# Feed-forward input products as seven half-size products for eight, in a two-layer encoder kernel

## The chip, the cores and the metric

The kernel runs on one core of one Trainium2 chip. The metric is device time in microseconds of one execution, the median of three runs. TensorE multiplies matrices, VectorE and ScalarE work element by element, GpSimd does a little of the same, and SyncE issues all transfers from main memory.

## The reference

512 tokens of width 1024 pass through two layers. Layer 0 mixes tokens with two kinds of heads, layer 1 with an mLSTM. Each is followed by the feed-forward part that this change is about:

```python
def conv_glu_ffn(h, w_in, conv_w, conv_b, w_out):
    u = jnp.matmul(h, w_in)              # (512, 1024) x (1024, 2 * 2816)
    a, g = jnp.split(u, 2, axis=-1)
    a = causal_dwconv(a, conv_w, conv_b) # 3 taps along the tokens
    return jnp.matmul(jax.nn.gelu(a) * g, w_out)

x = x + g_f * conv_glu_ffn(modulate(x, norm_ffn_g, sh_f, sc_f), ...)
```

The modulation (shift, scale, gate) of each sub-layer is a product of `c` with `ada_w`, 6 x 1024 columns for each layer.

## The kernel before

Activations lie transposed: a tile holds 128 channels in its partitions and 512 tokens along it. Every matmul takes 32-bit operands in a rounded form (`F32R`). To keep the precision each operand is split in a high part and a low part, and `mm3` issues three products: high by high, high by low, low by high. Weights are split on chip, in `load_split`: SyncE loads a raw piece of 128 x 2048, ScalarE rounds it to the high part (line 212), VectorE subtracts to get the low part (line 213). There are two raw buffers and three pairs of high and low.

The feed-forward part (`ffn`) has 22 tiles of 128 channels for `a` and 22 for `g`. They are made two at a time (a pair): 8 slices of the 1024 inputs, times two tiles, times `a` and `g`, times three products, is 96 matmuls of 128 x 512. The first pair is done in two halves of 256 tokens, because the second half of the tokens is normalized while the first is multiplied (`Handoff`, `modulate`). Behind the products of a tile stands a chain of its own: ScalarE (line 1038), two taps on VectorE (1040, 1042), GELU on ScalarE (1047), the product with `g` on VectorE (1048), and the split (219, 220). After 8 tiles their output product is added to `x` (8 blocks, `x_update`, line 351), after 16 again, and the last 6 go through `halves_out`, which ends the layer in two halves of 256 tokens and feeds the next norm.

The modulation columns (`ada_many`, line 170) are VectorE reductions over 128 x 1024 raw weights, 96 of them in the kernel. They are put between other work: 24 in the mixer of layer 0 (after 16 at its start), 48 in the feed-forward part of layer 0, 8 in that of layer 1.

A scheduler sets the order on each engine from the dependencies and the program's order; each engine then runs its list strictly in that order. Tile pools decide when a buffer is free.

## Time and profile before

| what | us |
|---|---|
| median of 3 runs | 1295.5 (1294.74 to 1295.51) |
| the profiled execution, its own time | 1296.03 |
| its span, first to last instruction | 1294.3 |
| TensorE busy | 1261.4 |
| VectorE busy | 797.7 |
| ScalarE busy | 471.9 |

The busy time of an engine is the union of its instructions. Matmuls overlap: the time that one adds is the distance between the starts of two that follow each other, not its duration.

### The profile page before, as it was taken

What the parts mean: (1) busy time and instruction counts of PE and PEld (TensorE: products, weight loads), DVE (VectorE), ACT (ScalarE), POOL (GpSimd) and SP (SyncE); (2) the same over time, 40 slices, a digit from 0 to 9 for tenths busy, and PEclk for the clock granted to TensorE, in tenths of its full rate; (3) what the DMA queues carried; (4) which work ended last, traced back from release to release, by engine and by line L of the source; (5) the groups of instructions that cost most, each with busy time, mean ns of one, the idle gap of its engine ahead of it and who ended that gap; (6) DMA issues with size and microseconds to landing.
All of it is one profiled execution on the core that took longest, in us unless ns stands there. A gap on an engine that the chain in (4) does not pass through costs nothing.

```text
span 1294.3 us, 16057 instructions
## 1 busy us (share of the span) xinstructions
PE 1261.4 (97%) x6390; PEld 1046.6 (81%) x6390; DVE 797.7 (62%) x1213; ACT 471.9 (36%) x734; POOL 114.4 (9%) x199
## 2 busy tenths in 40 slices
PE   5999999999999999999999999999999999999997
PEld 4866788899888888888898777779988888888887
DVE  7845678757865477447665846567875335443555
ACT  4454323125321132212346665774522122221321
POOL 0022154401000000000000120111000000000000
PEclk9999999999999999999999999999999999999998
DMA  8832635221664356434423203111162313222221
GB/s 316 293 105 82 212 98 195 87 77 66 218 206 143 128 204 225 146 130 159 169 91 128 78 21 104 59 66 66 66 212 70 126 65 125 71 100 96 82 74 66
DMA packets 33242, 162.47 MB, mean 126 GB/s; under 512 B 3600, under 2 KB 6032, under 8 KB 21648
## 3 DMA queue, kind: packets, MB, share of 16 engines
q1 hardware_dynamic: 33168, 161.46, 36.6%
q8 instruction: 50, 0.82, 0.3%
q14 instruction: 24, 0.20, 0.0%
HBM read 159.35 MB, written 2.10 MB: 125 GB/s over the span
## 4 chain that ended last, share of the span: by engine, by line
PE 86%; issue 7%; DVE 2%; POOL 2%; DMA 1%; ACT 1%; SPq 0%; POOLq 0%; DVEq 0%; ACTq 0%
PE acc L224 20%; PE acc L226 20%; PE acc L225 20%; PE mx L225 5%; PE mx L224 5%; PE mx L226 5%; PE mx L455 2%; PE acc L260 1%; PE acc L262 1%; PE acc L261 1%; PE mx L859 1%; PE mx L885 1%; PE mx L500 1%; DMA wraw<-wflat 1%; PE mx L550 1%
## 5 line engine op out<-in xcount | busy, mean ns | idle before, releaser
L224 PE MATMUL acc<-hh,wah 128*128 128x512 f32 (+1 forms) x384 | 145.0, 378 | 0.1
L226 PE MATMUL acc<-hh,wgl 128*128 128x512 f32 (+1 forms) x384 | 144.7, 377 | 0.0
L226 PE MATMUL acc<-hh,wal 128*128 128x512 f32 (+1 forms) x384 | 144.5, 376 | 0.0
L224 PE MATMUL acc<-hh,wgh 128*128 128x512 f32 (+1 forms) x384 | 144.3, 376 | 0.0
L225 PE MATMUL acc<-hl,wgh 128*128 128x512 f32 (+1 forms) x384 | 144.2, 376 | 0.0
L225 PE MATMUL acc<-hl,wah 128*128 128x512 f32 (+1 forms) x384 | 144.1, 375 | 0.0
L170 DVE CUSTOM_DVE_ANT_0 adaraw<-adaraw,csb,par 128x1024 f32<-128x1024 f32 x96 | 123.5, 1289 | 2.3 <-DMA adaraw<-adaT 2.3
L213 DVE TENSOR_TENSOR wl<-wraw,wh 128x2048 fp32r<-128x2048 f32 (+1 forms) x40 | 87.2, 2179 | 50.1 <-ACT wh L212 50.0
L224 PE MATMUL acc<-hh,wh 128*128 128x512 f32 x256 | 104.9, 410 | 0.0
L226 PE MATMUL acc<-hh,wl 128*128 128x512 f32 x256 | 101.4, 396 | 0.0
L225 PE MATMUL acc<-hl,wh 128*128 128x512 f32 x256 | 101.4, 396 | 0.0
L225 PE MATMUL mx<-actl,wdh 128*128 128x512 f32 x256 | 101.2, 395 | 0.0
L224 PE MATMUL mx<-acth,wdh 128*128 128x512 f32 x256 | 101.1, 395 | 0.0
L226 PE MATMUL mx<-acth,wdl 128*128 128x512 f32 x256 | 100.8, 394 | 0.0
L212 ACT CAST wh<-wraw 128x2048 fp32r<-128x2048 f32 (+1 forms) x40 | 72.0, 1801 | 64.8 <-PE acc L225 59.2
L212 ACT CAST wgh<-wgraw 128x2048 fp32r<-128x2048 f32 x22 | 42.0, 1907 | 139.5 <-PE acc L225 102.5
L213 DVE TENSOR_TENSOR wgl<-wgraw,wgh 128x2048 fp32r<-128x2048 f32 x22 | 50.4, 2292 | 66.4 <-ACT wgh L212 66.4
L307 POOL TENSOR_TENSOR nr<-nv,mhalf 128x2 f32<-128x2 f32 (+1 forms) x9 | 11.9, 1318 | 817.7 <-ACT nv L305 817.7
L224 PEld LDWEIGHTS acc<-hh,wah 128*128 128x128 f32 x384 | 72.3, 188 | 14.6 <-ACT hh L346 0.5
L225 PEld LDWEIGHTS acc<-hl,wgh 128*128 128x128 f32 x384 | 72.2, 188 | 14.5
L225 PEld LDWEIGHTS acc<-hl,wah 128*128 128x128 f32 x384 | 72.2, 188 | 14.3
L226 PEld LDWEIGHTS acc<-hh,wgl 128*128 128x128 f32 x384 | 72.2, 188 | 14.3
(261 smaller groups left out, 2624.0 us busy)
## 6 DMA issues: line engine op xcount, KB each, us to landing
adaraw<-adaT SPq DMA_DIRECT2D x96, 512.0 KB, 4.5
wraw<-wflat SPq DMA_DIRECT2D x30, 1024.0 KB, 5.0
waraw<-wflat SPq DMA_DIRECT2D x22, 1024.0 KB, 5.0
wgraw<-wflat SPq DMA_DIRECT2D x22, 1024.0 KB, 4.9
wdraw<-wflat SPq DMA_DIRECT2D x16, 1024.0 KB, 5.1
wraw<-wflat SPq DMA_DIRECT2D x10, 768.0 KB, 4.3
wraw<-wflat SPq DMA_DIRECT2D x8, 512.0 KB, 5.8
x<-xT SPq DMA_DIRECT2D x8, 256.0 KB, 5.0
```

The source lines that it names most:

```text
L170: return nc.vector.tensor_tensor_reduce(out=tile_, in0=tile_, in1=csb, scale=1.0, scalar=pc("ada_b", o), op0=ALU.mult, op1=ALU.add, accum_ ...
L212: nc.scalar.copy(hi, raw)
L213: nc.vector.tensor_sub(lo, raw, hi.bitcast(F32))
L224: nc.tensor.matmul(out, ah, bh, start=start, stop=False)
L225: nc.tensor.matmul(out, ah, bl, start=False, stop=False)
L226: nc.tensor.matmul(out, al, bh, start=False, stop=stop)
L260: nc.tensor.matmul(ps, ah[:, ts], wh[:, k % 4, :], start=(k == 0), stop=False)
L261: nc.tensor.matmul(ps, ah[:, ts], wl[:, k % 4, :], start=False, stop=False)
L262: nc.tensor.matmul(ps, al[:, ts], wh[:, k % 4, :], start=False, stop=(k == KD - 1))
L455: nc.tensor.matmul(lps[:, c * 64:(c + 1) * 64].rearrange("p (b m) -> p b m", m=m), k[:, s], qu, start=True, stop=True)
L500: nc.tensor.matmul(ops[:, c * P:(c + 1) * P], lt, va[s][:, hs], start=(n == 0), stop=(n == len(terms) - 1))
L550: nc.tensor.matmul(ops[:, kb * P:], vb[kb][:, hs], AT[kb][:, kb * P:], start=(kb == 0), stop=(kb == NCH - 1), skip_group_check=True)
```

## The change

From the fifth tile on, two tiles of `a` (or of `g`) are one block of 256 channels x 1024 inputs times 1024 inputs x 512 tokens. Each factor is cut in four quarters, and the block is made from seven products of quarters rather than eight (Winograd's form of Strassen's product). Class `Seven` holds a block: X is `a`, Y is `g`. A product is 4 slices x 3 matmuls of 128 x 256, so 84 for a block and 168 for a pair of tiles, called a set below; there are nine sets in a layer. The products are named X1 to X7 and Y1 to Y7.

- The weight sums are made on VectorE from raw weights (`prep`: four sums of 128 x 512 for each block), and then split. A block has 3584 columns to split rather than 2048.
- The token side (`tokens_side`) needs the normalized input unrounded (`modulate_halves` keeps it as `hfull`), four sums of 128 x 256 and two splits for each of four slices. It is done once in a layer, during the second pair.
- Partial results go through PSUM banks: bank a takes products 1, 6, 7 and 4 one after the other, and is read between them (`run`). So X4 can't start before VectorE has read X7's sum from that bank, and X6 not before ScalarE has read X1's.
- All weights come in pieces of 1024 columns: four raw buffers, ten tiles for high and low parts (five pairs; the blocks of a set need six), four small ones for product 4, three for sums.
- Output products come after 6, 4, 4 and 4 tiles, and 4 are left for `halves_out`. They are put into the sets that begin with tiles 6, 10 and 14, and after the last set.
- The rounding of the activations moves from VectorE to ScalarE (`split_act`).
- The modulation columns are moved: 32 in the mixer of layer 0, 24 in the feed-forward part of layer 0, 24 in the mixer of layer 1 (which had none), none in the last feed-forward part.

```diff
-    NW, NR, NS, NA = 43, 2, 3, 3
+    NW, NR, NS, NQ, NX, NA = 42, 4, 10, 4, 3, 2
...
+    def sum_tile(name):
+        return rawp.tile([P, D], F32, tag="sums", name=nm(name), bufs=NX)
+
+    def w_tiles(n, name):
+
+        if n <= T:
+            return tuple(wsp.tile([P, T], F32R, tag="wq", name=nm(name), bufs=NQ)[:, :n] for _ in range(2))
+        return tuple(wsp.tile([P, D], F32R, tag="ws", name=nm(name))[:, :n] for _ in range(2))
...
+    def load_split(src, kn, cols, name="w"):
+        ku = D // cols
+        pieces = []
+        wname, i, r0, r1, c0, c1 = src
+        for k0 in range(0, kn, ku):
+            k1 = min(k0 + ku, kn)
+            raw = raw_tile(name + "raw")[:, :(k1 - k0) * cols]
+            load(raw, [(wname, i, r0 + k0 * P, r0 + k1 * P, c0, c1)])
+            pieces.append(split_w(raw, name))
+        return Split(cols, ku, pieces)
...
-        nc.vector.tensor_copy(hi, src)
+        nc.scalar.copy(hi, src)
...
+            hi, lo = h[j][hf] = hl[:, 0, :], hl[:, 1, :]
+            nc.scalar.activation(hi, t1, AF.Identity, bias=sh)
+            nc.scalar.activation(t1, t1, AF.Identity, bias=sh)
+            nc.vector.tensor_sub(lo, t1, hi.bitcast(F32))
...
-        side = ada_many(0, range(4, 10))
+        side = ada_many(0, range(4, 12))
...
-        cov = spread(cover(), side, 40, 5)
+        cov = spread(cover(), side, 40, 4)
...
-        cov = cover()
+        cov = spread(cover(), ada_many(1, range(6, 12)), 0, 5)
...
+    ORDER = ("X1", "X5", "Y1", "Y5", "X6", "Y6", "X2", "X7", "Y2", "Y7", "X3", "X4", "Y3", "Y4")
+    PREPS = ("X1", "X5", "X7", "X4", "Y1", "Y5", "Y7", "Y4")
+    OUT_AT, LEAD, FETCH = 4, 8, 13
...
+        def fetch(self):
+            self.raw = [raw_tile(self.name + "raw") for _ in range(2)]
+            for m in range(2):
+                load(self.raw[m], [self.w[:, self.c0 + m * P:self.c0 + (m + 1) * P]])
+
+        def prep(self, n):
+            (a11, a12), (a21, a22) = ((r[:, 0:T], r[:, T:D]) for r in self.raw)
+            if n == 1:
+                src, ns = self.raw[0], (1, 2)
+            elif n == 5:
+                src, ns = sum_tile(self.name + "s"), (5, 6)
+                self.s2 = src[:, T:D]
+                nc.vector.tensor_add(src[:, 0:T], a21, a22)
+                nc.vector.tensor_sub(self.s2, src[:, 0:T], a11)
+            elif n == 7:
+                src, ns = sum_tile(self.name + "s"), (7, 3)
+                nc.vector.tensor_sub(src[:, 0:T], a11, a21)
+                nc.vector.tensor_sub(src[:, T:D], a12, self.s2)
+            elif n == 4:
+                src, ns = a22, (4,)
+            else:
+                return
+            hi, lo = split_w(src, self.name)
+            for i, m in enumerate(ns):
+                self.pieces[m] = hi[:, i * T:(i + 1) * T], lo[:, i * T:(i + 1) * T]
+
+        def run(self, n):
+            r = {1: "a", 6: "a", 7: "a", 4: "a", 5: "b", 3: "b", 2: "c"}[n]
+            first = n in (1, 5, 2)
+            if first:
+                self.ps[r] = (ps_mx() if r == "c" else ps_acc())[:, :256]
+            ps = self.ps[r]
+            hi, lo = self.pieces.pop(n)
+            for kk in range(4):
+                ks = slice(kk * P, (kk + 1) * P)
+                bh, bl = self.bs[n][kk]
+                nc.tensor.matmul(ps, hi[:, ks], bh, start=first and kk == 0, stop=False, skip_group_check=True)
+                nc.tensor.matmul(ps, hi[:, ks], bl, start=False, stop=False, skip_group_check=True)
+                nc.tensor.matmul(ps, lo[:, ks], bh, start=False, stop=kk == 3, skip_group_check=True)
+            a = self.ps["a"]
+            if n == 1:
+                self.p = wt("pp", [P, 2, 256])
+                nc.scalar.copy(self.p[:, 0, :], a)
+            elif n == 5:
+                nc.scalar.copy(self.p[:, 1, :], ps)
+            elif n == 6:
+                self.u2 = wt("u2")[:, :256]
+                nc.scalar.copy(self.u2, a)
+            elif n == 2:
+                self.v[0] = wt("v")
+                nc.vector.tensor_add(self.v[0][:, 0:256], ps, self.p[:, 0, :])
+            elif n == 7:
+                self.v[1] = wt("v")
+                nc.vector.tensor_add(self.v[1][:, 256:512], a, self.p[:, 1, :])
+            elif n == 3:
+                nc.vector.tensor_add(self.v[0][:, 256:512], ps, self.u2)
+            else:
+                nc.scalar.copy(self.v[1][:, 0:256], a)
...
-        groups = ((0, 8), (8, 8), (16, 6))
+        groups = ((0, 6), (6, 4), (10, 4), (14, 4), (18, 4))
...
+        def tokens_side(kk):
+            f0, f1 = hand.full[kk], hand.full[kk + 4]
+            b11, b12, b21, b22 = f0[:, 0:256], f0[:, 256:512], f1[:, 0:256], f1[:, 256:512]
+            u = wt("tu", [P, 2, 256])
+            v = wt("tv", [P, 2, 256])
+            nc.vector.tensor_sub(u[:, 0, :], b12, b11)
+            nc.vector.tensor_sub(v[:, 0, :], b22, b12)
+            nc.vector.tensor_sub(u[:, 1, :], b22, u[:, 0, :])
+            nc.vector.tensor_sub(v[:, 1, :], b21, u[:, 1, :])
+            for t, ns in ((u, (5, 6)), (v, (7, 4))):
+                hi = wt("th", [P, 2, 256], dt=F32R)
+                lo = wt("tl", [P, 2, 256], dt=F32R)
+                nc.scalar.copy(hi, t)
+                nc.vector.tensor_sub(lo, t, hi.bitcast(F32))
+                for i, n in enumerate(ns):
+                    bs[n][kk] = hi[:, i, :], lo[:, i, :]
+            bs[1][kk] = h[kk][0]
+            bs[2][kk] = h[kk + 4][0]
+            bs[3][kk] = h[kk + 4][1]
...
+        for f0 in (0, 2):
+            wa = load_split(w[:, f0 * P:f0 * P + 256], 8, 256, "wa")
+            wg = load_split(w[:, F + f0 * P:F + f0 * P + 256], 8, 256, "wg")
...
+        def set_jobs(fi, outs):
+            blocks = {"X": Seven(w, fi * P, bs, "wa"), "Y": Seven(w, F + fi * P, bs, "wg")}
+
+            def post():
+                take(2)
+                for s in range(2):
+                    act_g(act_a(fi + s, blocks["X"].v[s]), blocks["Y"].v[s])
+
+            for i, name in enumerate(ORDER):
+                if i == OUT_AT and outs is not None:
+                    out_jobs(outs)
+                b, n = blocks[name[0]], int(name[1])
+                p = PREPS[i] if i < len(PREPS) else None
+                jobs.append((blocks[p[0]].fetch if p and p[1] == "1" else None,
+                             (lambda p=p: blocks[p[0]].prep(int(p[1]))) if p else None,
+                             lambda b=b, n=n: b.run(n), post if i == len(ORDER) - 1 else None))
+
+        for fi in range(4, NF, 2):
+            set_jobs(fi, {6: 0, 10: 1, 14: 2}.get(fi))
+        out_jobs(3)
+        nf = npr = 0
+        for j, (_, _, run, post) in enumerate(jobs):
+            while nf < min(j + FETCH, len(jobs)):
+                if jobs[nf][0]:
+                    jobs[nf][0]()
+                nf += 1
+            while npr < min(j + LEAD, len(jobs)):
+                if jobs[npr][1]:
+                    jobs[npr][1]()
+                npr += 1
+            run()
...
-        yield from ada_many(0, (10, 11))
-        yield from ada_many(1, range(10))
+        yield from ada_many(1, range(6))
...
-    ffn(1, hand, ada_many(1, (10, 11)), fin)
+    ffn(1, hand, iter(()), fin)
```

How the rows stand on the engines. First VectorE in the feed-forward part of layer 0 before the change, from a pair of tiles without an output product; `cv` is the chain's tile, `wgl` a low part of `g` weights, `adaraw` a modulation column.

```order
L1040 SCALAR_TENSOR_TENSOR cv_3579<-acc_3551,par,cv_3579 128x511
L1042 SCALAR_TENSOR_TENSOR cv_3579<-acc_3551,par,cv_3579 128x510
L170 ISA adaraw_3608,mod<-adaraw_3608,csb,par 128x1024
L170 ISA mod 128x1
L1048 TENSOR_TENSOR cv_3579<-cv_3579,acc_3583 128x512
L219 CAST acth_3613<-cv_3579 128x512
L220 TENSOR_TENSOR actl_3614<-cv_3579,acth_3613 128x512
L170 ISA adaraw_3642,mod<-adaraw_3642,csb,par 128x1024
L170 ISA mod 128x1
L213 TENSOR_TENSOR wgl_3694<-wgraw_3692,wgh_3693 128x2048
```

And what stands there now, in the set of tiles 16 and 17 of layer 0: `v` are the sums read from PSUM (the first from product 2, the next from product 7), `was` and `wgs` weight sums, `wa` and `wg` low parts, for the set of tiles 18 and 19.

```order
L223 TENSOR_TENSOR wa_5619<-was_5615,wa_5618 128x1024
L1135 TENSOR_TENSOR v_5595<-mx_5582,pp_5501 128x256
L223 TENSOR_TENSOR wa_5641<-was_5637,wa_5640 128x1024
L1138 TENSOR_TENSOR v_5613<-acc_5488,pp_5501 128x256
L1135 TENSOR_TENSOR v_5635<-mx_5622,pp_5534 128x256
L1138 TENSOR_TENSOR v_5656<-acc_5521,pp_5534 128x256
L1101 TENSOR_TENSOR wgs_5712<-wgraw_5578,wgraw_5579 128x512
L1102 TENSOR_TENSOR wgs_5712<-wgraw_5578,wgs_5692 128x512
L1140 TENSOR_TENSOR v_5595<-acc_5503,u_1019_5562 128x256
L223 TENSOR_TENSOR wg_5676<-wgraw_5578,wg_5675 128x1024
L1160 SCALAR_TENSOR_TENSOR cv_5738<-v_5595,par,cv_5738 128x511
L223 TENSOR_TENSOR wa_5659<-waraw_5518,wa_5658 128x512
```

What was a chain and one split for a tile is now a mixture of sums, splits of 1024 and reads of PSUM that all wait in one list: the second `v` row, which frees bank a for X4, stands behind the split of a weight.

TensorE where the first set of layer 0 begins, after (the last number of a name tells tiles apart; `acc_665` is bank b of X, `acc_670` bank b of Y, `th` and `tl` are the token side, 3298 and 3299 its last slice).

```order
L1121 MATMUL acc_670_3412<-th_622_3176,wg_656_3349 128x256
L1122 MATMUL acc_670_3412<-tl_623_3177,wg_656_3349 128x256
L1123 MATMUL acc_670_3412<-th_622_3176,wg_657_3350 128x256
L1121 MATMUL acc_665_3379<-th_633_3298,wa_646_3327 128x256
L1121 MATMUL acc_670_3412<-th_633_3298,wg_656_3349 128x256
L1122 MATMUL acc_665_3379<-tl_634_3299,wa_646_3327 128x256
L1123 MATMUL acc_665_3379<-th_633_3298,wa_647_3328 128x256
L1122 MATMUL acc_670_3412<-tl_634_3299,wg_656_3349 128x256
L1123 MATMUL acc_670_3412<-th_633_3298,wg_657_3350 128x256
L1121 MATMUL acc_663_3364<-th_588_3000,wa_646_3327 128x256
```

Before, the rows of the third pair stood here, six of which are these:

```order
L224 MATMUL acc_2878<-hh_2476,wah_2867 128x512
L225 MATMUL acc_2878<-hl_2477,wah_2867 128x512
L226 MATMUL acc_2878<-hh_2476,wal_2868 128x512
L224 MATMUL acc_2878<-hh_2482,wah_2867 128x512
L225 MATMUL acc_2878<-hl_2483,wah_2867 128x512
L226 MATMUL acc_2878<-hh_2482,wal_2868 128x512
```

They needed only `hh` and `hl`, made long before; now the products 5, 6, 7 and 4 of both blocks need the four slices of the token side. VectorE makes the last slice of them here:

```order
L1101 TENSOR_TENSOR was_3509<-waraw_3393,waraw_3394 128x512
L223 TENSOR_TENSOR wa_3470<-waraw_3393,wa_3469 128x1024
L251 TENSOR_TENSOR actl_3289<-cv_3282,acth_3288 128x512
L1190 TENSOR_TENSOR tu_3292<-hfull_2615 128x256
L1191 TENSOR_TENSOR tv_3293<-hfull_2639,hfull_2615 128x256
L1192 TENSOR_TENSOR tu_3292<-hfull_2639,tu_3292 128x256
L1102 TENSOR_TENSOR was_3509<-waraw_3393,was_3487 128x512
L1193 TENSOR_TENSOR tv_3293<-hfull_2639,tu_3292 128x256
L1198 TENSOR_TENSOR tl_3299<-tu_3292,th_3298 128x512
```

Before, none of these rows was there; the row of `tl_3299` is the 67th that VectorE runs from the first pair's chain on, and TensorE's first row that reads it the 69th of the first set.

## Rows read from the trace of the kernel before

**Rows 1.** The page, part 1: busy time and share of each engine.

```profile
PE 1261.4 (97%) x6390; PEld 1046.6 (81%) x6390; DVE 797.7 (62%) x1213; ACT 471.9 (36%) x734; POOL 114.4 (9%) x199
```

**Rows 2.** Stretches of the span: us, busy time (instructions) per engine, PEclk, DMA.

```profile
300.00:324.50 24.50, 24.49 (x205) 24.16 (x204) 18.88 (x36) 12.53 (x21) 3.87 (x1) 1.00 0.23 86
346.00:640.00 294.00, 293.97 (x1278) 237.70 (x1277) 183.33 (x228) 74.47 (x64) 0.00 (x0) 1.00 0.51 172
975.00:1250.00 275.00, 275.00 (x1188) 221.88 (x1187) 123.28 (x127) 70.21 (x60) 0.00 (x0) 1.00 0.27 92
112.00:300.00 188.00, 183.76 (x1081) 157.68 (x1080) 132.74 (x223) 56.85 (x124) 60.02 (x83) 1.00 0.38 124
715.00:860.00 145.00, 141.05 (x678) 109.35 (x676) 91.53 (x173) 94.07 (x190) 22.67 (x54) 1.00 0.19 66
```

**Rows 3.** TensorE in order of time, layer 0, products of 512 columns, first and last.

```profile
500.20 0.39 PE L224 MATMUL acc<-hh,wgh 128*128 128x512 f32 x1
...
507.17 0.39 PE L224 MATMUL acc<-hh,wah 128*128 128x512 f32 x1
```

**Rows 4.** TensorE in order of time, products of 256 columns, first and last.

```profile
319.73 0.28 PE L225 MATMUL acc<-hl,wah 128*128 128x256 f32 x1
...
324.10 0.28 PE L226 MATMUL acc<-hh,wgl 128*128 128x256 f32 x1
```

**Rows 5.** VectorE groups by shape: count | busy us, mean ns | idle before.

```profile
L170 DVE CUSTOM_DVE_ANT_0 adaraw<-adaraw,csb,par 128x1024 f32<-128x1024 f32 x96 | 123.5, 1289 | 2.3 <-DMA adaraw<-adaT 2.3
...
L220 DVE TENSOR_TENSOR actl<-cv,acth 128x512 fp32r<-128x512 f32 x44 | 30.5, 693 | 1.5
...
L351 DVE SCALAR_TENSOR_TENSOR x<-mx,mod,x 128x512 f32<-128x512 f32 x32 | 24.0, 750 | 90.8 <-PE mx L226 90.8
...
L606 DVE TENSOR_TENSOR w<-wraw,w 128x1024 fp32r<-128x1024 f32 x8 | 9.7, 1218 | 0.7 <-ACT w L602 0.7
...
L282 DVE TENSOR_TENSOR sqa<-sq,sq 128x256 f32<-128x256 f32 x8 | 3.4, 420 | 1.5 <-ACT sq L275 1.4
```

**Rows 6.** VectorE in order of time at 28 us, a stretch without a gap.

```profile
28.60 0.69 DVE L610 TENSOR_TENSOR xr<-x,rb 128x512 f32<-128x512 f32 x1
29.20 1.22 DVE L606 TENSOR_TENSOR w<-wraw,w 128x1024 fp32r<-128x1024 f32 x1
30.34 1.28 DVE L170 CUSTOM_DVE_ANT_0 adaraw<-adaraw,csb,par 128x1024 f32<-128x1024 f32 x1
...
31.55 0.68 DVE L619 TENSOR_TENSOR hl<-xr,hh 128x512 fp32r<-128x512 f32 x1
```

**Rows 7.** VectorE in order of time, the first pair of layer 0 and after.

```profile
318.96 0.75 DVE L1040 SCALAR_TENSOR_TENSOR cv<-acc,par,cv 128x511 f32<-128x511 f32 x1 [1.56 <-ACT cv L1038]
...
322.53 0.69 DVE L1048 TENSOR_TENSOR cv<-cv,acc 128x512 f32<-128x512 f32 x1 [2.04 <-ACT cv L1047]
...
328.40 0.74 DVE L1042 SCALAR_TENSOR_TENSOR cv<-acc,par,cv 128x510 f32<-128x510 f32 x1
329.06 2.28 DVE L213 TENSOR_TENSOR wal<-waraw,wah 128x2048 fp32r<-128x2048 f32 x1
331.26 0.68 DVE L1048 TENSOR_TENSOR cv<-cv,acc 128x512 f32<-128x512 f32 x1
```

**Rows 8.** The stretch after the last matmul: busy time, PEclk 0.50.

```profile
1288.00:1294.30 6.30, 0.00 (x0) 0.00 (x0) 3.20 (x8) 0.00 (x0) 0.00 (x0) 0.50 0.50 166
```

**Rows 9.** TensorE after the first wait of the kernel, in order of time.

```profile
20.03 2.07 PE L626 MATMUL acc<-w,hh 128*128 128x512 f32 x4 [1.63 <-ACT hh L615]
21.91 1.91 PE L628 MATMUL mx<-hh,w 128*128 128x512 f32 x4
...
24.92 1.09 PE L628 MATMUL mx<-hh,w 128*128 128x512 f32 x4
```

**Rows 10.** The chain that ended last, in the even layer: start, us, what.

```profile
127.61 1.20 DVE adaraw L170
128.85 4.38 DMA adaraw<-adaT
```

More of the change, by code (lines that the diff above doesn't have):

```diff
@@ L320, in __init__ @@
             self.layer, self.which = layer, which
-            self.h = [None] * KD
+            self.h = [[None, None] for _ in range(KD)] if which else [None] * KD
+            self.full = [None] * KD
             self.st = [None, None]
@@ L1051, in mms, with half_products @@
-        def mms(ps, wt_, sl, ts):
+            nc.vector.tensor_mul(c0t, c0t, g)
+            acts.append(split_act(c0t, "act"))
+        def half_products(ps, ws_, sl, hf):
             for k in range(KD):
-                mm3(ps[:, ts], wt_[0][:, k, sl], wt_[1][:, k, sl], h[k][0][:, ts], h[k][1][:, ts], k == 0, k == KD - 1)
+                mm3(ps[:, hf * 256:hf * 256 + 256], *ws_.get(k, sl), *h[k][hf], k == 0, k == KD - 1)
+                yield 1
         def first_half(pss, wa, wg):
             for hf in range(2):
-                ts = slice(hf * 256, hf * 256 + 256)
+                for s in range(2):
+                    for ps, ws_ in ((pss[s][0], wa), (pss[s][1], wg)):
+                        yield from half_products(ps, ws_, slice(s * P, (s + 1) * P), hf)
@@ new lines, in ffn @@
+        bs = {n: [None] * 4 for n in range(1, 8)}
+        def tokens_side(kk):
[17 more added lines that the diff above has]
+            bs[3][kk] = h[kk + 4][1]
@@ L1058, in first_half @@
+        for f0 in (0, 2):
+            wa = load_split(w[:, f0 * P:f0 * P + 256], 8, 256, "wa")
+            wg = load_split(w[:, F + f0 * P:F + f0 * P + 256], 8, 256, "wg")
+            if f0 == 0:
+                pss = [(ps_acc(), ps_acc()) for _ in range(2)]
+                drain(first_half(pss, wa, wg), hand.hooks(1, 6, 15))
+                for s in range(2):
+                    act_g(act_a(s, pss[s][0]), pss[s][1])
+                    tokens_side(s)
+            else:
                 for s in range(2):
@@ new lines, in ffn, with out_jobs, prep, run @@
+                    ps = ps_acc(), ps_acc()
+                    for i, ws_ in enumerate((wa, wg)):
+                        for hf in range(2):
+                            drain(half_products(ps[i], ws_, sl, hf))
+                    act_g(act_a(f0 + s, ps[0]), ps[1])
+                    tokens_side(f0 + s)
+            take(2)
+        jobs = []
+        def out_jobs(gi):
+            f0, fn = groups[gi]
+            for cb in range(4):
+                st = {}
+                def prep(cb=cb, st=st):
+                    st["w"] = load_split(wd[f0 * P:(f0 + fn) * P, cb * 256:(cb + 1) * 256], fn, 256, "wd")
+                def run(cb=cb, st=st):
@@ L1096, in ffn @@
                         for k in range(fn):
-                            mm3(ps, wo[0][:, k, sl], wo[1][:, k, sl], acts[k][0], acts[k][1], k == 0, k == fn - 1)
+                            mm3(ps, *st["w"].get(k, sl), *acts[f0 + k], k == 0, k == fn - 1)
                         x_update(ps, layer, 1, cb * 2 + s)
-            else:
-                drain(side)
-                drain(halves_out(wd, f0 * P, fn, acts, layer, 1, out, 0, 2))
+                jobs.append((None, prep, run, None))
+        def set_jobs(fi, outs):
+            blocks = {"X": Seven(w, fi * P, bs, "wa"), "Y": Seven(w, F + fi * P, bs, "wg")}
+            def post():
+                take(2)
+                for s in range(2):
+                    act_g(act_a(fi + s, blocks["X"].v[s]), blocks["Y"].v[s])
[21 more added lines that the diff above has]
+            run()
+            if post:
+                post()
+        drain(side)
+        drain(halves_out(wd, 18 * P, 4, acts[18:], layer, 1, out, 0, 2))
     HG_STEP, SB_STEP, ML_STEP, HG_T, SB_T, ML_T, ML_A = 2, 2, 3, 5, 2, 3, 4
```

142 lines of the change are left out of this document (64 added, 78 removed).

## The prediction

> **What bounds the kernel now.** The page's busy shares come first: TensorE works 1261.4 of 1294.3 us [rows 1]. Then the stretches, since a share is a mean over stages. In the feed-forward parts TensorE never stops (293.97 of 294.00 us, 275.00 of 275.00; the first pair 24.49 of 24.50), while VectorE is busy 183.33 and 123.28 us there; in the mixers TensorE idles 4.24 of 188 and 3.95 of 145 us [rows 2]. So inside the feed-forward parts a matmul saved is time saved, as long as nothing else takes TensorE's place; VectorE, 62% busy, is the next engine. The third view is the order of starts, because matmuls and VectorE instructions overlap their neighbours.
>
> **TensorE's part of the change.** Between 500.20 and 507.17 lie 30 matmuls of 512 columns, .2323 us each [rows 3]; between 319.73 and 324.10 lie 37 of 256 columns, .1181 us [rows 4], a little more than half. A pair costs 96 × .2323 = 22.30 us, a set 168 × .1181 = 19.84: 2.46 saved, in 18 sets 44.3. The second pair, now in half products, takes 192 × .1181 = 22.68, .38 more, twice. Together **−43.5**.
>
> **What VectorE gets.** Its groups give durations [rows 5], but instructions overlap. Start to start, where it has no gap: a 512-wide operation .60 us (28.60 to 29.20), a 1024-wide 1.14, a modulation column 1.21 [rows 6], with its short second row some 1.29; the operation with three inputs .66 at 512 (329.06 less 328.40), the split of 2048 2.20 [rows 7]. For 256 wide I take .34, an estimate: its duration .420 less the .08 by which a 1024-wide duration, 1.218, exceeds its step [rows 5, 6]. A set of layer 0 then puts on VectorE 6 splits of 1024 (6.8), 14 operations of 512 (8.4: eight weight sums, two splits of sums, two products with g, two activation splits), 4 taps (2.6), 6 reads of PSUM (2.0) and 2 columns (2.6): 22.4 us. Layer 1 has no columns: 19.8. Each chain also waits for ScalarE at the GELU and the rounding, some .75 twice a set (estimate). So 24 and 21.3 against TensorE's 19.84: VectorE is 4.1 and 1.5 behind in a set without output products. Output products of four tiles give TensorE 96 × .2323 = 22.3 us for 8 updates of x at .66 and four more splits of 1024, 9.8 us: 12 us for VectorE to catch up.
>
> **Start of the first set.** The token side sits in VectorE's list between the chains of the first two pairs and the weight sums. From the first pair's chain to the last `tl` row that TensorE needs, VectorE runs 67 rows in layer 0: 10 of 1024, 29 of 512, 8 taps, 16 of 256, 2 columns, 42.1 us, with the first GELU's 2.04 wait [rows 7] 44.1. In layer 1, without columns, 42.7. TensorE has meanwhile 60 matmuls left of the first pair less ScalarE's .78 ahead of the chain (6.3), the second pair (22.7) and 68 matmuls of the set (8.0): 37.0. So it waits 7 and 6 us for the last slice, **+13** (4 and 4 if VectorE's waits vanish and small operations are cheaper; 11 and 10 if each is dearer as by duration).
>
> **The sets.** In-order lists turn lateness into TensorE's wait at two places: X4 and Y4, which need bank a after VectorE has read product 7's sum (the second `v` row, behind a 1024-wide split), and output products, whose operands are the chain of the set before. Layer 0: a set with output products repays what the set ahead of it lost, so lone sets 8 and 12 lose little (2.5 each, of 4.1), and sets 16, 18 and 20 come in a row (12.3 behind at worst; I take half): **+11** (0 if the queue has enough lead, 20.5 if all of it lands on TensorE). Layer 1: **+2** of at most 7.5.
>
> **Other terms.** [...] After TensorE's first wait 12 matmuls take 4.89 us (20.03 to 24.92) instead of 2.79 [rows 9]: a wait can cost 2.1 more. One of the two long waits: **+2** (0 to 6). ScalarE gets the rounding of the activations and a second pass in the hand-over; it has 12.53 us of work in 24.5 at the first pair [rows 2], and `halves_out` with four tiles rather than six hides less: **+2** (0 to 4). The mixer of layer 1 gets 24 columns, 31 us of VectorE, which is busy 91.53 of 145 [rows 2]; a column stood on the chain once, 1.20 with its transfer of 4.38 [rows 10], and the other mixer carries its columns with as little idle TensorE: **+2** (0 to 6); eight more columns in that one **+1** (0 to 3). Each column brings its transfer along in SyncE's queue; the DMA engines are busy .19 of the layer 1 mixer and .38 of the other [rows 2], so those fit, and the feed-forward parts lose them. Pieces of 1024 cost two times 1.14 for 2.20: nothing on TensorE's path while VectorE's own sum above is what counts; the transfers, .51 of the DMA engines at most [rows 2], rise by no raw bytes. Five pairs of weight tiles for six needed make the sixth split wait for TensorE's last use; it is in the lateness taken.
>
> **Sum.** −43.5 + 13 + 11 + 2 + 2 + 2 + 2 + 1 = −10.5 against the profiled execution's 1296.0, which stands .5 above the median: 1285.5, and **1285** for the median. With all terms low (starts 8, the rest 0) it is −35.5, with all high (21, 28, 6, 4, 6, 3) +24.5.
>
> **Rivals.** *VectorE keeps up.* Its list runs ahead as far as tiles allow, five pairs of low parts and three of sums; if it builds a lead during output products, sets flow at 19.84, the starts cost 10 and the rest 5: −28.5, about 1267. For it: 183.33 of 294 us busy now, so there is room; against it: the columns still stand in this list in layer 0, and nothing is removed from the sets but 24 columns.
>
> *VectorE's list sets the pace (slower).* Bank a must be read twice and ScalarE once inside each block, and each read stands behind work for the next set. If TensorE waits 2 us in every set, with or without output products, that is 18 × 2 = 36 instead of 13: 1296.0 − 43.5 + 13 + 7 + 36 − .5 = 1308. It turns into a loss at (43.5 − 13 − 7) / 18 = 1.3 us a set; the forecast has 13 / 18 = .7. A single 1024-wide split ahead of a read is 1.14 and a column 1.21 [rows 6], so one such row at the wrong place in each set nearly decides. For it: 22.4 against 19.84 by the sums; against it: Y2, Y7 and X3 stand between X7 and X4, 36 matmuls or 4.3 us of cover for the read.
>
> *Small pieces cost their whole duration (slower).* If VectorE's instructions didn't overlap, a set would take it 25.3 and 22.5 us by the durations of [rows 5], with the waits 6.9 and 4.2 more than TensorE; the terms of the sets grow in that proportion to 18.5 and 5.6, the starts go to 21, and the time is 1296.0 − 43.5 + 21 + 18.5 + 5.6 + 7 − .5 = 1304. The rows without a gap [rows 6] speak against it. [...]
>
> *The clock falls at the waits.* If each of some twelve waits brings the slow start of [rows 9], 12 × 2.1 = 25 instead of 2: about 1308. The trace shows a lower granted clock only after TensorE's work has ended [rows 8]; within the stretches it is 1.00 [rows 2]. [...]
>
> **How the numbers follow.** Chances: the forecast with its own range, 1277 to 1294, .45; VectorE keeps up, .20; VectorE's list sets the pace, .15; small pieces, .07; clock, .06; gain and waits equal, .07. A measurement of this kernel tells .2%, 2.6 us, from no change. Faster by more than that takes the forecast's part below 1293 (.35) and all of the second: .55; slower takes the three slow rivals (.28), .02 of the ties and .02 of the forecast: .32; within it, .13. The range of 8 in 10 runs from 1269, a little above the case where VectorE keeps up, to 1303, which cuts off the greater part of the slow rivals.
>
> **What would show it.** In the changed kernel TensorE's busy time should fall by 40 to 44 us, less what slow-clocked stretches add, and each set without waits should span 19.8 us. A wait of some 6 us for VectorE (`tl`) should stand on TensorE's rows in the first set of either layer, and waits of 1 to 4 us ended by `v` reads or `cv` and `act` rows around sets 8, 12 and 16 to 20 of layer 0, fewer in layer 1. VectorE should be over 90% busy between the first set and the last of layer 0. The forecast fails if VectorE shows gaps there while TensorE waits (then a buffer or ScalarE sets the order), if small operations cost VectorE clearly other than .34, .60 and 1.14, if waits appear in each set, or if the granted clock falls below 1.00 inside the feed-forward parts.

## The result, and the profile after

The changed kernel takes 1313.3 us (1311.6 to 1314.7), the kernel before 1295.5: ratio 1.0139, 95% interval 1.0116 to 1.0162. It is 1.4% slower; 1285 with a range of 1269 to 1303 was forecast.

The page's first part answers to [rows 1]: TensorE's busy time fell by 18.5 us where 43.5 were forecast, and its idle time in the span rose from 32.9 to 68.7.

```profile
PE 1242.9 (95%) x7782; PEld 1096.0 (84%) x7782; DVE 1005.1 (77%) x1657; ACT 638.4 (49%) x1151; POOL 113.2 (9%) x199
```

Next the stretches of the changed kernel, with columns as in [rows 2]: the feed-forward part of layer 0 from its first input product to its last output product, the mixer of layer 1, the feed-forward part of layer 1; then two stretches, each from product 3 of one set to product 3 of the next: the first holds set 6 up to there, with its four blocks of output products, the second set 8, which has none. Below these two stretches are called set 6 and set 8.

```profile
299.34:682.20 382.86, 363.31 (x2543) 336.89 (x2542) 316.73 (x485) 184.09 (x299) 2.31 (x3) 0.97 0.38 124
682.20:924.00 241.80, 235.94 (x1207) 188.80 (x1206) 183.45 (x364) 154.53 (x315) 36.41 (x77) 1.00 0.36 118
924.00:1301.40 377.40, 361.77 (x2542) 336.31 (x2540) 288.52 (x436) 179.68 (x293) 2.25 (x2) 0.98 0.27 87
371.70:425.90 54.20, 54.16 (x315) 46.58 (x314) 35.66 (x52) 20.43 (x30) 0.00 (x0) 1.00 0.36 116
425.90:453.10 27.20, 22.28 (x170) 21.98 (x169) 23.93 (x36) 13.43 (x22) 0.00 (x0) 0.87 0.36 117
```

The same three stretches of the kernel before:

```profile
300.15:672.40 372.25, 372.21 (x1847) 311.52 (x1846) 241.06 (x323) 108.85 (x117) 4.63 (x3) 1.00 0.47 161
672.40:911.30 238.90, 234.95 (x1207) 189.16 (x1207) 156.19 (x306) 144.58 (x284) 32.86 (x77) 1.00 0.22 76
911.30:1284.50 373.20, 373.12 (x1849) 311.96 (x1847) 192.39 (x238) 103.02 (x109) 2.37 (x2) 1.00 0.28 97
```

From first to last matmul the feed-forward parts went from 372.0 and 372.9 to 382.6 and 377.2 us: 10.6 and 4.3 lost where 21.7 each should have been saved. The mixer of layer 1 lost 2.9, all the rest together gained .5. The fault lies in the feed-forward parts, in layer 1 too, where VectorE has no modulation columns. And in the last two rows: in set 6 VectorE is busy 35.7 of 54.2 us, in set 8 23.9 of 27.2 while TensorE stands idle for 4.9. What ended the idle time of VectorE (first) and ScalarE in set 6 (total, times, longest):

```profile
DVE wg L223 <- ACT wg L222: 6.6, 3, 2.9
DVE wd L223 <- ACT wd L222: 5.7, 5, 2.9
DVE was L1097 <- DMA waraw<-wflat: 2.4, 1, 2.4
DVE x L400 <- PE mx L257: 2.2, 1, 2.2
```

```profile
ACT wg L222 <- PE mx L256: 12.4, 3, 6.4
ACT wd L222 <- PE mx L256: 7.8, 4, 6.4
```

VectorE waits mostly for ScalarE's half of a split, and ScalarE for a weight tile that an output product still reads. In set 8 VectorE has one gap up to the end of TensorE's wait, .9 us: it is full.

TensorE's waits in the changed kernel (total, times, longest), those of the feed-forward parts that matter:

```profile
PE acc L1121 <- ACT pp L1127: 12.6, 6, 4.9
PE mx L1121 <- ACT wa L222: 7.6, 4, 2.6
PE acc L1121 <- DVE cv L1162: 5.4, 2, 2.8
PE acc L1121 <- ACT th L1197: 5.0, 3, 2.5
PE mx L256 <- DVE actl L251: 1.6, 2, 0.8
```

The third and fourth are the first sets; the largest, `pp`, is ScalarE's copy of bank a (line 1127), for which product 6 waits. VectorE's read before product 4, the forecast's place, comes to .4 us in all. The longest wait, in set 8 of layer 0, in order of time on TensorE, ScalarE and VectorE:

```profile
439.89 0.28 PE L1123 MATMUL mx<-hhl,wg 128*128 128x256 f32 x1
445.10 0.58 PE L1121 MATMUL acc<-th,wa 128*128 128x256 f32 x1 [4.92 <-ACT pp L1127]
445.48 0.41 PE L1122 MATMUL acc<-tl,wa 128*128 128x256 f32 x1
445.69 0.41 PE L1123 MATMUL acc<-th,wa 128*128 128x256 f32 x1
```

```profile
440.60 1.03 ACT L222 CAST wa<-waraw 128x1024 fp32r<-128x1024 f32 x1
444.16 0.62 ACT L250 CAST acth<-cv 128x512 fp32r<-128x512 f32 x1 [2.52 <-DVE cv L1168]
444.68 0.36 ACT L1127 COPY pp<-acc 128x256 f32<-128x256 f32 x1
```

```profile
439.89 1.22 DVE L223 TENSOR_TENSOR wg<-wgs,wg 128x1024 fp32r<-128x1024 f32 x1
441.03 1.28 DVE L169 CUSTOM_DVE_ANT_0 adaraw<-adaraw,csb,par 128x1024 f32<-128x1024 f32 x1
...
442.23 1.28 DVE L169 CUSTOM_DVE_ANT_0 adaraw<-adaraw,csb,par 128x1024 f32<-128x1024 f32 x1
...
443.44 0.69 DVE L1168 TENSOR_TENSOR cv<-cv,v 128x512 f32<-128x512 f32 x1
```

Read backwards: product 6 waits for the copy `pp`; the copy waits in ScalarE's list behind the rounding `acth`, which waits for VectorE's product with g, which stands behind a split and two modulation columns. Behind the wait the matmuls last .41 us and start .21 apart, at near half the pace of those ahead of it (.28 and .118). TensorE's granted clock in that place falls to .53 (third from the end; third row: 446 to 450 us):

```profile
438.00:442.00 4.00, 2.17 (x19) 1.97 (x17) 3.96 (x5) 2.62 (x3) 0.00 (x0) 1.00 0.00 0
442.00:446.00 4.00, 0.90 (x4) 0.90 (x5) 4.00 (x8) 1.71 (x5) 0.00 (x0) 0.62 0.60 168
446.00:450.00 4.00, 4.00 (x22) 4.00 (x21) 2.23 (x3) 1.32 (x2) 0.00 (x0) 0.53 0.58 225
450.00:454.00 4.00, 4.00 (x35) 3.91 (x34) 3.46 (x8) 1.32 (x2) 0.00 (x0) 1.00 0.01 4
```

The feed-forward parts' account, from the order of TensorE's rows: waits 19.2 and 15.4 us; matmuls at half pace (66 and 54 of them, each by what its step exceeds .118) 7.4 and 5.8; 10.6 is what is left of the 58.4 between −43.5 and the 10.6 + 4.3 = 14.9 measured. Of this remainder some 6 us stand at the 25 waits of over .15 us themselves: 4.4 for the last matmul ahead of each, which runs out, and some 2 for the first one behind, of .35 to .58 instead of .28 (.50 instead of .39 at 512 columns). The other 4 are gaps too small to be listed and single slow steps.

### The profile page after: what moved, and what is told of

Same layout as the page of the kernel before. It is cut to its first block, busy times and chain, and to the rows that moved or that the text cites. A ratio compares the mean times of both kernels' runs of the same rounds, so it can differ in the third digit from the quotient of the medians.

```text
span 1311.6 us, 20082 instructions
## 1 busy us (share of the span) xinstructions
PE 1242.9 (95%) x7782; PEld 1096.0 (84%) x7782; DVE 1005.1 (77%) x1657; ACT 638.4 (49%) x1151; POOL 113.2 (9%) x199
## 4 chain that ended last, share of the span: by engine, by line
PE 64%; DVE 16%; issue 9%; ACT 6%; DMA 2%; POOL 1%; SPq 0%; POOLq 0%; DVEq 0%; ACTq 0%
PE acc L255 8%; PE acc L256 8%; PE acc L257 7%; PE mx L256 5%; PE mx L257 5%; PE mx L255 5%; PE acc L1121 5%; PE acc L1122 4%; PE acc L1123 4%; DVE wg L223 2%; DVE wa L223 2%; PE mx L503 2%; PE acc L289 1%; PE acc L291 1%; PE acc L290 1%
## 5 line engine op out<-in xcount | busy, mean ns | idle before, releaser
L256 PE MATMUL mx<-actl,wd 128*128 128x512 f32 x288 | 113.4, 396 | 1.6 <-DVE actl L251 1.6
L255 PE MATMUL mx<-acth,wd 128*128 128x512 f32 x288 | 112.8, 397 | 0.4 <-ACT acth L250 0.4
L257 PE MATMUL mx<-acth,wd 128*128 128x512 f32 x288 | 112.9, 395 | 0.0
L255 PE MATMUL acc<-hh,w 128*128 128x512 f32 x256 | 105.2, 411 | 0.0
L1121 PE MATMUL acc<-th,wa 128*128 128x256 f32 x288 | 85.7, 298 | 18.1 <-ACT pp L1127 12.6
L223 DVE TENSOR_TENSOR w<-wraw,w 128x1024 fp32r<-128x1024 f32 x68 | 83.9, 1240 | 23.1 <-ACT w L222 13.4
L257 PE MATMUL acc<-hh,w 128*128 128x512 f32 x256 | 101.3, 396 | 0.0
L256 PE MATMUL acc<-hl,w 128*128 128x512 f32 x256 | 101.1, 395 | 0.0
L222 ACT CAST w<-wraw 128x1024 fp32r<-128x1024 f32 x68 | 71.2, 1050 | 61.0 <-PE acc L256 29.3
L1121 PE MATMUL acc<-th,wg 128*128 128x256 f32 x288 | 85.0, 295 | 0.1
L1122 PE MATMUL acc<-tl,wa 128*128 128x256 f32 x288 | 84.1, 292 | 0.7 <-DVE tl L1198 0.6
L1123 PE MATMUL acc<-th,wa 128*128 128x256 f32 x288 | 83.9, 291 | 0.0
L1122 PE MATMUL acc<-tl,wg 128*128 128x256 f32 x288 | 83.3, 289 | 0.0
L1123 PE MATMUL acc<-th,wg 128*128 128x256 f32 x288 | 82.7, 290 | 0.0
L222 ACT CAST wd<-wdraw 128x1024 fp32r<-128x1024 f32 (+1 forms) x40 | 38.5, 967 | 63.9 <-PE mx L256 35.7
```

Source lines behind the costliest of these rows:

```text
L222: nc.scalar.copy(hi, src)
L223: nc.vector.tensor_sub(lo, src, hi.bitcast(F32))
L255: nc.tensor.matmul(out, ah, bh, start=start, stop=False)
L256: nc.tensor.matmul(out, ah, bl, start=False, stop=False)
L257: nc.tensor.matmul(out, al, bh, start=False, stop=stop)
L1121: nc.tensor.matmul(ps, hi[:, ks], bh, start=first and kk == 0, stop=False, skip_group_check=True)
```

## Experiments

Four theories. **A**, order of the lists: the copy that frees bank a stands behind the rounding, which the change moved to ScalarE. **B**, load: VectorE has more work in a set than TensorE. **C**, no carry-over: in sets with output products VectorE is held (by full weight tiles, by `x` rows that wait for TensorE) and can't work ahead, so each set without them is late by what VectorE's load in it exceeds TensorE's; it keeps B's load and denies that other sets repay it. **Clock**: each wait is followed by a stretch at half the clock, a cost of its own. Times are medians against 1313.3; every run stands beside the kernel before, at 1295.1 to 1295.7. The parts are those of the profiled execution, from first to last matmul.

| kernel | us | ratio to before, 95% | part of layer 0 | part of layer 1 |
|---|---|---|---|---|
| before | 1295.5 | | 372.0 | 372.9 |
| changed | 1313.3 | 1.0116 to 1.0162 | 382.6 | 377.2 |
| e1_late_chain | 1317.1 | 1.0158 to 1.0198 | 389.9 | 377.6 |
| e2_round_dve | 1313.7 | 1.0121 to 1.0154 | 389.0 | 373.9 |
| e3_ada_out | 1317.7 | 1.0157 to 1.0188 | 389.0 | 375.3 |
| e4_sums_pool | 1339.9 | 1.0331 to 1.0362 | 397.1 | 387.8 |
| e7_pairs4 | 1318.0 | 1.0160 to 1.0190 | 389.2 | 376.5 |
| e8_pairs6 | 1326.2 | 1.0224 to 1.0258 | 391.2 | 369.2 |
| e9_pairs5 | 1330.2 | 1.0248 to 1.0288 | 390.0 | 378.1 |
| e12_lead12 | 1336.2 | 1.0295 to 1.0326 | 405.9 | 377.3 |
| e6_spread | 1278.7 | 0.9855 to 0.9888 | 367.1 | 360.0 |
| e10_spread_ada | 1271.0 | 0.9794 to 0.9823 | 356.9 | 359.9 |
| e11_fill | 1310.2 | 1.0102 to 1.0136 | 381.2 | 376.6 |

### e1_late_chain: the copies ahead of the chain

```diff
...
-            if post:
+            if late and j == late[0]:
+                late.pop()()
+                late.clear()
+            if post and j + 5 < len(jobs) and j + 1 not in outs_at and j + 5 not in outs_at:
+                late[:] = j + 4, post
+            elif post:
                 post()
```

> The chain of a set whose next set has no output products (the sets before 8, 12, 16, 18 and 20 of either layer) is issued after that next set's products 1 and 5 instead of before them, so that ScalarE's copies of bank a (pp) stand ahead of the GELU and the rounding in its list. Theory A (the lists of ScalarE and VectorE wait for each other: pp stands behind a rounding that waits for VectorE's chain): the six waits for pp, 12.6 us, go to under 2, with them some 4 us of slow clock and 2 us of restarts, so about 1313 - 17 = 1296. Theory B (VectorE has simply more work in a set, 22.4 and 19.8 us and its waits, than TensorE's 19.84): the same work in another order, the waits move to other rows, 1309 to 1316.

1317.1 us. A's forecast falls: the waits for `pp` are gone, and this line of the waits has taken their place, for the copy `u` that frees the bank one product later and now stands behind the chain.

```profile
PE acc L1121 <- ACT u L1132: 27.3, 8, 4.5
```

In this order TensorE waits at another place, and no less; one with all copies ahead of the chain was not tried. In layer 0 moreover each of the four waits of 3.1 to 4.5 us is followed by matmuls at half pace (13.1 us with the first set's).

### e2_round_dve: the rounding back on VectorE

```diff
-        nc.scalar.copy(hi, src)
+        nc.vector.tensor_copy(hi, src)
```

> The rounding of activations goes back from ScalarE to VectorE, as in the kernel before, where such a row took .42 us. Theory A (pp waits behind the rounding in ScalarE's list): ScalarE no longer waits there for VectorE's product with g; the waits for pp fall by half, the GELU still stands ahead of them: about 1313 - 6 = 1307. Theory B (VectorE's load): VectorE gets .34 us more per tile, .7 per set, so the sets without output products (five in each layer) lose .7 each and the first sets 1.4 each: 1313 + 10 = 1323 at most, 1317 to 1323.

1313.7 us, neither. The waits for `pp` fell to 5.4 us, as A said; others rose (8.7 us for a low part of `wa` from VectorE). Layer 1 gained 3.3 us, layer 0 lost 6.4: that VectorE, with columns in its list, pays for the rows it takes back and without them has room is a reading that no run tests.

### e3_ada_out: the columns behind output blocks

```diff
-            take(2)
-
...
                         x_update(ps, layer, 1, cb * 2 + s)
+                    take(2)
...
             def post():
-                take(2)
```

> The 24 modulation columns in the feed-forward part of layer 0 are moved from behind the pairs and sets to the output products, two behind each of the first twelve blocks of 256. Theory B (VectorE's load): sets 8, 12, 16, 18 and 20 and the first set lose 2.6 us of VectorE's work each, where TensorE waits now 5.3 + 4.9 + 1.9 + 2.0 + 2.6 + .9 us; about 12 us of waits and the slow clock behind two of them, 5 us, go: 1313 - 17 = 1296. Theory A (a queue order in which the columns are only one of the rows ahead of the chain): layer 0 falls to what layer 1, without columns, waits now: 19.2 to 16.3 us, 1313 - 5 = 1308.

1317.7 us: neither forecast came. With no column in its chain, set 8 still waits 4.2 us for `pp`, set 12 4.1, layer 1's sets as before. But the run takes no work from VectorE. The columns now stand in the sets with output products, and work that was done there comes later: from product 1 of set 8 to product 1 of set 10 VectorE is busy 22.3 us, in the changed kernel 23.3, so that .9 of the 2.6 us were gained. It does not decide between load and order.

### e4_sums_pool: the weight sums on GpSimd

```diff
-                nc.vector.tensor_sub(src[:, 0:T], a11, a21)
-                nc.vector.tensor_sub(src[:, T:D], a12, self.s2)
+                nc.gpsimd.tensor_sub(src[:, 0:T], a11, a21)
+                nc.gpsimd.tensor_sub(src[:, T:D], a12, self.s2)
```

(and the two of product 5 alike)

> The weight sums, eight of 128 x 512 in each set, go from VectorE to GpSimd, which has nothing to do in the feed-forward parts. VectorE's sum for a set falls by 4.8 us to 17.6 and 15.0. Theory B (VectorE's load): all waits between sets go, 14 us in layer 0 and 11 in layer 1, with 9 us of slow clock: 1313 - 34 = 1279. Theory A (order of the lists): the chain has fewer rows ahead of it, but the rounding ahead of pp and the columns stay: waits halve, 1313 - 15 = 1298. If a sum takes GpSimd over 2.3 us, its list is longer than a set (8 x 2.3 = 18.4) and the time goes up instead.

1339.9 us. A sum took GpSimd some 1.3 to 2.2 us (1.28 to 1.67 in the four rows at 357 to 365 us), eight of them some 14 us a set, under the limit named, and the time rose all the same. It tells little of A and B, since the work that was moved slowed what stayed. VectorE by shape (count, busy us, mean ns), first the changed kernel, then this one:

```profile
L223 DVE TENSOR_TENSOR wa<-was,wa 128x1024 fp32r<-128x1024 f32 x36 | 43.7, 1216 | 9.8 <-ACT wa L222 9.7
...
L1160 DVE SCALAR_TENSOR_TENSOR cv<-v,par,cv 128x511 f32<-128x511 f32 x36 | 26.8, 744 | 0.1
...
L1138 DVE TENSOR_TENSOR v<-acc,pp 128x256 f32<-128x256 f32 x36 | 15.0, 416 | 1.5 <-PE acc L1123 1.4
```

```profile
L223 DVE TENSOR_TENSOR wa<-was,wa 128x1024 fp32r<-128x1024 f32 x36 | 62.3, 1732 | 3.6 <-ACT wa L222 3.6
...
L1160 DVE SCALAR_TENSOR_TENSOR cv<-v,par,cv 128x511 f32<-128x511 f32 x36 | 35.0, 973 | 0.2
...
L1138 DVE TENSOR_TENSOR v<-acc,pp 128x256 f32<-128x256 f32 x36 | 15.0, 416 | 1.1 <-PE acc L1123 1.0
```

In the mean the split is 42% longer, the tap 31%; the row that reads PSUM takes .416 us in both, though 19 of its 36 run wholly beside a sum. A tap that runs wholly beside one takes 1.77 us (8 of 36), the others .745. What makes them slower beside GpSimd these rows do not show.

### e7, e8, e9, e12: weight tiles and look-ahead

```diff
-    NW, NR, NS, NQ, NX, NA = 42, 4, 10, 4, 3, 2
+    NW, NR, NS, NQ, NX, NA = 42, 4, 8, 4, 3, 2
```

in e7_pairs4; in e8_pairs6 NS, NX and NA are 12, 2 and 1, in its control e9_pairs5 10, 2 and 1. In e12_lead12 instead:

```diff
-    OUT_AT, LEAD, FETCH = 4, 8, 13
+    OUT_AT, LEAD, FETCH = 4, 12, 17
```

> Four pairs of weight tiles instead of five, nothing else. Theory C (full weight tiles stop ScalarE's and VectorE's splits in sets with output products): everything is split later, more waits in all sets: over 1313 + 15 = 1328. Theory B (VectorE's load alone): its work is the same and mostly not ahead anyway: 1313 to 1318.

> Six pairs of weight tiles instead of five; to make room two tiles for weight sums instead of three and one for modulation columns instead of two. To be read against the run with the same two cuts and five pairs. Theory C: 10 to 20 us faster than that one. Theory B: within 3 us of it.

> The control for the run with six pairs: five pairs, two tiles for weight sums, one for modulation columns. One tile for columns makes VectorE wait for each transfer (4.3 us) where columns follow each other, in the mixers above all; both theories: slower than 1313, by 3 to 15.

> The changed kernel, whose list prepares weights 12 jobs ahead of TensorE's product rather than 8, and fetches them 17 ahead rather than 13; five pairs of weight tiles as before. If only the list's order keeps VectorE from working ahead while output products run (8 jobs ahead is all of that set's own weights): VectorE's idle 10 us between 400 and 440 us fill, the lone sets come in time: about 1313 - 20 = 1293. If the tiles do (there is nowhere to put the split weights): ScalarE and VectorE stand longer at full tiles, 1311 to 1325.

1318.0, 1326.2, 1330.2 and 1336.2 us. A pair of tiles less costs 4.7 us, not 15, and not where C had it: there is no wait for `pp` at all, the sets without output products follow each other faster, and the time is lost elsewhere (3.4 and 3.5 us alone in the first pairs, which wait for a high part of `wg`). Set 8 of either layer in e7_pairs4, from product 1 to product 1, columns as in [rows 2]:

```profile
438.39:461.23 22.84, 21.08 (x170) 20.20 (x169) 22.39 (x33) 13.23 (x23) 0.00 (x0) 1.00 0.43 137
...
1066.22:1087.51 21.29, 20.82 (x171) 20.15 (x169) 20.69 (x31) 13.55 (x22) 0.00 (x0) 1.00 0.29 99
```

Sets 12, 16 and 18 of layer 0 read alike. VectorE is busy nearly throughout, by 22.4 and 20.7 us where the forecast's sum has 22.4 and 19.8: here its list sets the pace, and set 6 has repaid nothing.

A pair more gives 4.0 against its control, not 10 to 20, and the ranges of the two runs overlap; layer 1, which has no columns, gains 8.9 (378.1 to 369.2), layer 0 loses 1.2. In set 6 of layer 0 VectorE stands idle as long as with five pairs (busy 36.3 of 54.2 us), with 8.3 us of it before `x` rows, 6.8 in the control and 2.2 in the changed kernel. So tiles are a part of what holds VectorE, not the whole. Looking further ahead is worse than both branches said, in layer 0 alone (405.9; layer 1 377.3): two waits for `pp` grow to 9.4 and 7.8 us. VectorE is busy 33.5 of 54 us there from 371 to 425, as idle as before: the rows that stand earlier in its list have no tile to go to, and what stands behind them comes later.

### e6_spread: output products in every set

```diff
-        groups = ((0, 6), (6, 4), (10, 4), (14, 4), (18, 4))
+        groups = ((0, 4), (4, 4), (8, 4), (12, 4), (16, 2))
...
-            set_jobs(fi, {6: 0, 10: 1, 14: 2}.get(fi))
-        out_jobs(3)
+            c = fi % 4 // 2
+            set_jobs(fi, (fi // 4 - 1, range(2 * c, 2 * c + 2) if fi < 20 else range(4)))
```

> The output products are cut in groups of 4, 4, 4, 4 and 2 tiles and spread: two blocks of 256 columns in each set from 4 to 18, four small ones in set 20, instead of four in sets 6, 10, 14 and behind 20; halves_out unchanged. TensorE has then 31 us in every set against 27.3 (layer 0) and 24.7 (layer 1) of VectorE with 1.5 of waits. Theory C (the lateness does not carry over: in sets with output products VectorE is held up by full weight tiles and by x rows that wait for TensorE, idle 10 us between 400 and 440 us, so what it could catch up is lost, and sets without them are late each time): waits of the sets, some 14 and 10 us, and the slow clock behind them go, and the first set gains cover: about 1313 - 35 = 1278. Theory A or B as they stood: nothing is taken from VectorE's list and 5 us are added for two more groups of updates: 1305 to 1318.

1278.7 us, as C expected, and 1.3% faster than the kernel before, with 16 updates of `x` more. All waits for `pp`, `wa` and `cv` in the feed-forward parts are gone; the first sets, now with output products as cover for the token side, wait .2 us. What is left in the sets is 3.3 and 1.8 us, in waits of .2 to .8, and one place waits longer, the start of `halves_out` in layer 0 (4.8 us, with 2.6 us at half pace). The edit does two things at once: it evens out the load, and it puts some 11 us of TensorE's work between the products of every set, which would cover a long chain too. No run separates the two; that load alone is enough to hold a set without output products is what e7_pairs4 shows. VectorE at the start of `halves_out`, in the last chain:

```profile
633.63 1.28 DVE L169 CUSTOM_DVE_ANT_0 adaraw<-adaraw,csb,par 128x1024 f32<-128x1024 f32 x1
...
634.84 1.28 DVE L169 CUSTOM_DVE_ANT_0 adaraw<-adaraw,csb,par 128x1024 f32<-128x1024 f32 x1
...
636.04 0.69 DVE L1168 TENSOR_TENSOR cv<-cv,v 128x512 f32<-128x512 f32 x1
```

### e10_spread_ada: and the columns off the chain

The edit of e3_ada_out on top of e6_spread.

> The kernel with spread output products, and the 24 modulation columns of layer 0 moved from behind the pairs and from inside the chains to behind the output blocks of sets 4 to 14, two behind each block. There the last chain of the layer had two columns (2.6 us) between GELU and product and two more ahead of the first x rows, and TensorE waited .7 + 2.3 + 1.5 us at the start of halves_out with 2.6 us of slow clock behind it. If the columns in VectorE's list cause these: about 1279 - 6 = 1273. If the chain's own length does (layer 1, without columns, waits 1.3 there): 1277 to 1280.

1271.0 us, ratio .9809: the fastest kernel here. The same edit that cost 4 us in the changed kernel gives 8 in this one. Its feed-forward parts, in the columns of [rows 2], with the clock at 1.00 in both and VectorE 90% busy in layer 0:

```profile
298.90:656.10 357.20, 354.18 (x2543) 329.42 (x2542) 319.88 (x494) 186.14 (x299) 2.29 (x3) 1.00 0.42 133
...
897.30:1257.40 360.10, 356.49 (x2542) 330.00 (x2540) 293.87 (x444) 180.47 (x293) 2.26 (x2) 1.00 0.28 91
```

The sets of layer 0 follow each other every 31.2 to 31.7 us (404.17 to 435.36, the first matmuls of product 3). A set and two blocks of output products should take 19.84 + 48 × .2323 = 30.99 by the forecast's rows: where next to nothing waits, the seven products save what was forecast but for .2 to .7 us a set. The two feed-forward parts together are 28.1 us shorter than before, of 43.5; what is missing is the waits that are left, their starts and small gaps.

### e11_fill: work in the waits

On top of e1_late_chain:

```diff
+            if n == 7 and self.w.index == 0 and self.c0 in (8 * P, 12 * P, 16 * P, 18 * P):
+                pf = ps_mx()[:, :256]
+                bh = self.bs[7][0][0]
+                for i in range(24):
+                    nc.tensor.matmul(pf, hi[:, 0:P], bh, start=i == 0, stop=i == 23, skip_group_check=True)
```

> The kernel with the late chain, and in sets 8, 12, 16 and 18 of layer 0 24 more matmuls of 256 columns (2.8 us, into a bank that nothing reads) ahead of product 7 of X, where TensorE waits 4.5, 4.5, 3.1 and 4.4 us for ScalarE and runs 1.4 + 1.4 + 2.7 + 2.8 us at half the clock's pace behind these waits. Clock theory (the half clock follows from the gap in TensorE's work, and its cost comes on top of the wait): the waits shrink to 1.7, 1.7, .3 and 1.6 at no cost, nothing behind them runs at half pace, about 1317 - 8 = 1309. Rival (the slow stretches are no cost of their own, since TensorE would wait again behind them): 1315 to 1319.

1310.2 us: 96 matmuls more, 11 us of work, and 6.9 us less than e1_late_chain. Around three of the waits (windows of 10 us, the granted clock third from the end), e1_late_chain first:

```profile
446.00:456.00 10.00, 5.48 (x34) 5.37 (x34) 8.02 (x15) 3.56 (x6) 0.00 (x0) 0.83 0.01 2
514.00:524.00 10.00, 5.47 (x36) 5.26 (x34) 8.02 (x14) 3.56 (x6) 0.00 (x0) 0.83 0.02 7
583.00:593.00 10.00, 6.89 (x38) 6.68 (x37) 7.76 (x13) 2.97 (x6) 0.00 (x0) 0.69 0.01 2
```

```profile
446.00:456.00 10.00, 8.29 (x70) 8.09 (x69) 9.08 (x16) 5.37 (x9) 0.00 (x0) 1.00 0.06 13
514.00:524.00 10.00, 8.28 (x70) 8.08 (x69) 9.07 (x17) 4.89 (x10) 0.00 (x0) 1.00 0.09 25
582.00:592.00 10.00, 9.81 (x83) 9.61 (x83) 8.86 (x15) 5.27 (x10) 0.00 (x0) 1.00 0.14 46
```

The waits shrank to 1.7, 1.7, .2 and .5 us and no matmul behind them ran at half pace. The clock theory holds (granted clock 1.00 in these windows, .69 to .83 in e1_late_chain): the slow stretch is a cost on top of the wait.

## Why the prediction was wrong

**TensorE's −43.5: right.** The sets' distance in e10_spread_ada shows it. In the changed kernel the matmuls outside the slow stretches kept the same pace, and the gain was eaten.

**Mixers and hand-overs, +5: near.** Layer 1's mixer lost 2.9 with its 24 columns (2 forecast); all the rest gained .5 (3 of loss forecast).

**Start of the first sets, +13: right.** The waits were 5.4 and 5.7 us, and the last `tl` row that TensorE needs starts 43.9 and 43.3 us behind the first chain's first row on VectorE, where 44.1 and 42.7 were forecast. The wait at the `tl` row itself was only .6 in all; TensorE stood earlier, at a PSUM bank that VectorE's taps still held (`cv`, 2.8 and 2.6) and at ScalarE's `th` of the same last slice. That the wait for the bank only takes the place of a longer one for the slice is argued, not tried.

**The sets, +11 and +2: the step that failed.** It read "a set with output products repays what the set ahead of it lost", and gave layer 1 almost nothing, since VectorE's 19.8 us nearly fit there. Waits in layer 0 were 13.4 us, near 11 by size, but in layer 1 9.2, over the 7.5 that it called the most. With the slow stretches and starts behind the waits, sets 8, 12, 16 and 18 took 24.2 us in the mean in layer 0 and 23.0 in layer 1, TensorE's 19.84 and all that VectorE was behind by the forecast (4.1 and 1.5) or more: next to nothing was repaid. The sum over VectorE's work held, by e7_pairs4; the 12 us that it has to spare while output products run were not to be had. In set 6 it stands idle for 18.5 of 54.2 us, and in set 8 it is full. e6_spread (same work, evenly laid, no such waits) and e7_pairs4 (VectorE's own pace in these sets) show it; e1_late_chain (another order, no fewer waits) fits. The forecast's sign, VectorE over 90% busy from the first set to the last of layer 0, failed too: 241.6 of 289.8 us, 83%.

What holds VectorE in set 6: in the changed kernel 12.3 us of its idle time end with ScalarE's half of a split, 2.4 with a transfer and 2.2 with a matmul that an `x` row waits for; ScalarE in turn waits 20.2 us for full weight tiles. In e8_pairs6 (six pairs of tiles) the idle time is as long and a greater part of it stands before `x` rows, so one limit stands behind the other. How much each alone costs stays open, and a longer look-ahead without more tiles costs 23 us.

**The place.** The forecast had X4 behind VectorE's `v` read; it was X6 behind ScalarE's copy, and product 2 behind ScalarE's split of `wa`. The forecast charged VectorE for its waits on ScalarE (an estimate of .75 us twice a set; set 6 shows .8 and .7), but not ScalarE's copy for the rounding's wait on VectorE: in set 8 of layer 0 that wait, 2.52 us, stood ahead of the copy and within the 4.92 us that TensorE waited for it.

**Clock, +2: mis-sized.** It was 13.2, about halfway between this and the 25 of the rival that had it at every wait. One of two long waits was charged; in fact both first sets and two of the later waits in each layer were followed by it (granted clock .53 behind the 4.92 us of set 8), and others were not (1.00 behind those of 1.87 and 1.84 us in sets 12 of the two layers). Its price of 2.1 a wait was of the right size (6.5 us for the four later ones), in part by luck: the trace before records the granted clock only from 24.4 us on, so [rows 9] do not tell whether it had fallen at that wait or been low since the kernel's start. That the lower clock follows from the gap in TensorE's work is what e11_fill shows: with matmuls in the gaps it was 1.00 in the three windows above.

**Waits' own starts: missing.** The 10.6 us of remainder had no term: a wait costs more than its listed length, by some 6 us in all at the 25 listed, and finer gaps add the rest.

The profiled executions are 17.3 us apart where −10.5 was forecast. Of these 27.8 us the waits are 8.6 (34.6 for 26), the clock 11.2, the starts and small gaps 10.6, and mixers and hand-overs give 2.6 back. So the two slow rivals came true at once, each in part. Without the first sets and their slow stretches (11.0 and 6.7) the 58.4 leave 40.7, 2.3 us a set, beyond the 1.3 at which the forecast's own rival turned into a loss.
